# RWKV's decay part of the next head pair is made ahead of this pair's inverse; the next delta head's keys are made under this head's chunk loop

## The chip, the core and the metric

The kernel runs on one NeuronCore of one Trainium2 chip. The metric is the device time of one execution in microseconds (us). The kernel before has a median of 2889.58 us over three runs (2887.1 to 2890.51). The profile that is read here is one execution taken by the hardware profiler; its span, from the first to the last instruction, is 2890.0 us.

## The reference, cut to what matters

One layer of a hybrid encoder works on 512 tokens of width 2048 in float32. One combined input projection feeds two groups of heads; their outputs are concatenated and projected, and cross attention to 256 memory tokens and a squared-ReLU MLP follow.

```python
y = rmsnorm(x) @ W_in                       # one projection for both groups
h = x + concat[GDN(y_gdn), RWKV7(y_rwkv)] @ W_out
h = h + CrossAttn(rmsnorm(h), rmsnorm(mem)) # 4 heads, 256 memory tokens
h = h + relu(rmsnorm(h) @ W_up)**2 @ W_down # hidden 8192
out = rmsnorm(h)

# RWKV-7, 16 heads of 64
w_log = -softplus(-(w0 + tanh(w_lo) @ w2)) - 0.5
decay = exp(-exp(w_log));  a = sigmoid(a0 + a_lo @ a2)
S_t = S_{t-1} (diag(decay_t) + a_t b_t^T) + v_t k_t^T;  o_t = S_t r_t

# gated DeltaNet, 8 heads of 128
q, k, v = silu(conv4(y))                    # q and k are then l2-normed
S_t = exp(g_t) (I - beta_t k_t k_t^T) S_{t-1} + beta_t k_t v_t^T;  o_t = S_t^T q_t
```

Both recurrences are computed in chunks: inside a chunk a unit triangular matrix is inverted, and a short loop over the chunks carries the state.

## The kernel before, in words

**Stages.** The first stage (0 to about 1120 us of the span) makes the input projection, both groups of heads, the key projection of the memory (`kp`) and its product with the query weights (`kq`). Then come the memory's values with the output weights (`vp`, `vo`), the mixer's output projection (`op`), attention (`sc`, `at`) and the MLP (`mxu`, `mgu`, `mmu`, then the tiles that end in `d`). The change lies in the first stage, and one line of it in the MLP.

**Precision.** Each float32 weight tile is split into a rounded part `whi` (ScalarE) and the rest `wlo` (VectorE), and so are the activations (`xhi`, `xlo`). A product then takes three matmuls. An output of the input projection takes 16 x 3 matmuls of 128x128 by 512 columns, tile `py`. There are 59 such outputs: three blocks of low ranks and rates, and then for each of eight rounds j three for a pair of RWKV heads (r, k, v, in this order) and four for one delta head (k, q, v, gate). `evict` (line 541) puts each into one of four buffers `y`, from which the heads take it.

**The order of the work.** It is planned while the program is built. Every piece of work is a Python generator that yields operations; `chain(generator, rank)` adds it to a list. `run` (line 285) repeatedly takes the next operation of each chain, works out by a cost model when it could start on its engine, and issues the one with the smallest start time, to which a rank adds 150 ns a step except on TensorE. `yield after(event)` holds a chain until another has issued the work that adds the event. The result is a fixed order for each engine: on the chip each engine takes its instructions in that order and waits for semaphores. The projections are one chain (`projections`, line 573, rank 4), so their matmuls fill TensorE wherever the heads' chains (rank 3) have nothing ready. `loader` (line 438) fetches weights into three `wraw` buffers over SyncE's DMA queue and splits them. `presums` (line 412, tile `ds`) makes sums of MLP weights ahead of time on VectorE where there is room, until the last `kp` is made.

**A pair of RWKV heads** is `rwkv(j)` (line 858). It begins with the decay part: two matmuls `pW` and `pA` of 64 rows by 512 columns, two Tanh on ScalarE, a scale and a scan (a running sum that restarts every 64 columns) on VectorE, and two Exp that give `E1` and `E2`; `tA` holds the second Tanh. Then k is mixed and normed (`pn`), r and v are mixed, the scaled operands `AR` and `BK` are made once the pair before has issued its output products (`after("po", j - 1)`), the chunk matrices `GA` and `GB` come from `pgA` and `pgB`, and a chain of its own inverts 16x16 blocks on GpSimd (`inverse_blocks`, tiles `sr`, over DRAM buffers `nd` and `bg`). Meanwhile this chain makes transposes and `pak`, `pkv`, and the tile `Qs`; it waits for the inverse (`after("ri", j)`), doubles the blocks twice (tiles `ri`), adds the chain of the next pair (`chain(rwkv(j + 1), 3)`, line 1029) and runs the chunk loop (`rs`) and the output products (`po`, `pp`).

**A delta head** is `gdn(h)` (line 1092). It loads the rates `B` (tile `gqd`), convolves k (three VectorE operations, tile `gk`), makes the decays `EG` and `E` (tiles `gEG`, `gE`) and the normed k (`gkn`, matmuls `gn`), then `pkk` and the matrix for the inverse, which again runs on GpSimd. q, v and the gate follow; after the inverse come the block steps (tiles `gi`), the event `("inverted", h)`, the chunk loop (`gs`), the output products (`gpo`), the output's norm (`gon`) and the store. Only as its last act does it add the chain of the next head (line 1237). `fetch` loads the next head's `E` earlier.

**What hangs on the last head.** The 16 outputs of `kp` come after the last input projection, and the first `kq` waits for the event `("inverted", 7)` (line 616), since `kq` uses PSUM banks that the delta head's block steps use.

Of the kernel before, what the change touches and what calls it, by code (L numbers as in the profile page):

```python
# [12 lines left out]
ALU = mybir.AluOpType  # L13
# [14 lines left out]
for _n, _w in (("ident", 128), ("ones", 128), ("mA", 128),  # L28
               ("lv64", 2 * 64), ("cen", 64), ("sneg", 128), ("mbias", 128),
               ("rst64", 512)):  # L30
    CST[_n] = (_off, _w)
    _off += _w
# [13 lines left out]
def constants():  # L46
    c = np.zeros((P, NCST), np.float32)

    def put(name, a):
        o, w = CST[name]  # L50
        c[:, o:o + w] = a

    i = np.arange(P)
    put("ident", np.eye(P))
    put("ones", 1.0)
    j = np.arange(64)
    st = (j[:, None] < j[None, :]).astype(np.float32)
# [12 lines left out]
    put("rst64", np.tile((np.arange(512) % 64 != 0).astype(np.float32), (P, 1)))  # L70
    return c


def build(tc, I, out):
# [43 lines left out]
    def psb(nm, tag="mx", bufs=2):  # L118
        return tile_of(ps, [P, 512], F32, tag, nm, bufs)
# [162 lines left out]
    def after(*ev):  # L282
        return lambda: ev in events
# [573 lines left out]

    def rwkv(j):
        base = 3 + 7 * j
        js = slice(j * P, (j + 1) * P)  # L860
# [66 lines left out]
        def store(full):  # L927
# [3 lines left out]
        inv = []  # L931
        chain(inverse_blocks(f"ri{j}", store, 16, ("k", "r", "E2"), lambda: (short(), short(240)), lambda: True, inv,
                             True), 1, ("ri", j))
# [36 lines left out]
        for f in (0, 1):  # L970
# [4 lines left out]
                         [prod(1 - h, h, pkv[:, CS[c]], Kt[:, CS[c]], VV[:, CS[c]]) for h, c in (L4 + H4)[:14]])  # L975
        AkV = tl("tA")
# [114 lines left out]

    def gdn(h):
        base = 3 + 7 * h + 3
        gsh = lambda w=512: short(w, "sg")
        c3 = lambda a: a.rearrange("p (c t) -> p c t", t=P)

        def conv(i, s, tag):

            yield after("py", base + i)
            y = ybuf[ys[base + i]]  # L1100
            a = tl(tag)
            cv = lambda i: hconv[:, (s * 8 + h) * 4 + i:(s * 8 + h) * 4 + i + 1]
            yield AC.activation(a, y[:, 0:512], AF.Copy, scale=cv(0))
            for n in range(1, 4):
                yield DV.scalar_tensor_tensor(out=a, in0=y[:, n:n + 512], scalar=cv(n), in1=a,
                                              op0=ALU.mult, op1=ALU.add)
            yfree.append(ys.pop(base + i))
            t = gsh()
            yield AC.activation(t, a, AF.Tanh)
            yield DV.scalar_tensor_tensor(out=a, in0=t, scalar=1.0, in1=a, op0=ALU.add, op1=ALU.mult)  # L1110
            return a

        def normed(x, bias, tag, nm):
            sq = gsh()
            yield AC.activation(sq, x, AF.Square)
            pn = psb(f"gn{h}_{nm}", "mg")
            yield from sums_(pn, onesr, sq)
            yield from rsq_(sq, pn, 1.0, b_eps6, bias)
            xn = tl(tag)
            yield DV.tensor_tensor(out=xn, in0=x, in1=sq, op=ALU.mult)  # L1120
            return xn
# [12 lines left out]
        eg = tl("eg", 4, 2)  # L1134
        yield DV.tensor_copy(eg.unsqueeze(2), c3(EG)[:, :, P - 1:P])
        for c in range(4):
# [15 lines left out]
        def store(full):  # L1152
# [5 lines left out]
                             after("gq", h), inv, moved=True), 1, ("gi", h))  # L1158
        q_ = yield from conv(1, 0, "gq")
        qn = yield from normed(q_, b_lq, "gqn", 1)  # L1160
        wd, qd = tl("gq"), B
# [17 lines left out]
        v_ = yield from conv(2, 2, "gv")  # L1179
        pvt = psb(f"pvt{h}", "mg")  # L1180
# [16 lines left out]
        events.add(("inverted", h))  # L1197
        vns, Ss = tl("gEs"), tl("gEG")
        for c in range(4):
# [35 lines left out]
        yield SL.dma_start(mixd[h], o)  # L1235
        if h < 7:
            chain(gdn(h + 1), 3)

# [694 lines left out]
    def splits():  # L1933
        for u in units:
            if u[0] == "d" and u[1:3] in INSITU and u[1:] not in PRE:
                for i, w in order_of(u):
                    for x in xs(u):
                        yield (after("sum", u, w, x) if isinstance(w, str) else after("raw", u, w, x))
                        r = raws[u, {"s2": A11, "s3": A21, "s4": A11 if u == units[-1] else A12}.get(w, w), x]
                        halves[u, i, x] = hl = yield from take(hfree)  # L1940
                        yield from cut(r, *hl)
                        events.add(("half", u, i, x))
                        if w not in (A11, "s2") and (w != A12 or u == units[-1]):
                            wfree.append(r)
                continue
# [520 lines left out]
```

## Time and profile before

| what | us |
|---|---|
| median of three runs | 2889.58 |
| lowest and highest run | 2887.1, 2890.51 |
| the profiled execution, span | 2890.0 |
| TensorE matmul busy in it | 2862.2 |
| VectorE busy | 2333.9 |
| ScalarE busy | 1571.7 |
| GpSimd busy | 214.7 |
| from first to last `kp` matmul | 907.2 to 1019.9 |
| from first to last `kq` matmul | 1022.3 to 1117.5 |

A matmul's record has a modelled end and overlaps the next one's, so the pitch from start to start says more than the duration. Idle time is counted from the modelled end of the matmul before. Each planner-issued instruction has the line of the helper that issues it (L257), so tiles, not lines, tell what an instruction is.

### The profile page before, as it was taken

The numbers are of one execution on the slowest core, as the hardware profiler recorded it, in microseconds if no ns is written. First come the engines' busy times: TensorE is split into PE (matmuls) and PEld (weight loads), VectorE is DVE, ScalarE is ACT, GpSimd is POOL, SyncE is SP. The second block draws the span as 40 slices with busy tenths as digits, with TensorE's granted clock in tenths as the row PEclk, the third lists the DMA queues.
The fourth block names the chain that finished last, engine by engine and source line by source line (L and its number), as shares of the span: only waits on it lengthen the run. The fifth ranks groups of instructions, "written<-read, shape, count | busy, mean of one in ns | idle before, by whom it ended". The sixth has DMA issues, their size and how long they took to land.

```text
span 2890.0 us, 49168 instructions
## 1 busy us (share of the span) xinstructions
PE 2862.2 (99%) x18794; PEld 2419.1 (84%) x18794; DVE 2333.9 (81%) x3559; ACT 1571.7 (54%) x2233; POOL 214.7 (7%) x539
## 2 busy tenths in 40 slices
PE   9999999999999999999999999999999999999998
PEld 7877887877877888889988888888888888888887
DVE  7787787787877877769956898899998878786888
ACT  6555555645656655664445556555555644454544
POOL 0213213213212100000000000000000000000000
PEclk9999999999999999999999999999999999999999
DMA  5656656657656788784422354666565878887733
GB/s 191 166 147 176 176 149 187 165 154 189 180 161 200 214 257 274 232 292 151 124 95 88 110 164 153 199 195 207 189 200 178 292 249 277 295 257 247 265 101 110
DMA packets 321212, 553.01 MB, mean 191 GB/s; under 512 B 101128, under 2 KB 188428, under 8 KB 320976
## 3 DMA queue, kind: packets, MB, share of 16 engines
q1 hardware_dynamic: 293584, 518.41, 58.7%
q10 hardware_dynamic: 27392, 31.46, 3.1%
q8 instruction: 147, 2.41, 0.3%
q14 instruction: 89, 0.73, 0.1%
HBM read 443.45 MB, written 106.31 MB: 190 GB/s over the span
## 4 chain that ended last, share of the span: by engine, by line
PE 94%; DMA 3%; DVE 1%; ACT 1%; issue 1%; ACTq 0%; SPq 0%; DVEq 0%
PE py L257 22%; PE mxu L257 12%; PE mgd L257 6%; PE mgu L257 6%; PE mxd L257 6%; PE op L122 6%; PE vp L122 3%; PE mmu L257 3%; PE sc L122 3%; PE at L122 3%; PE scrd L257 3%; PE scgd L257 3%; PE mmd L257 3%; PE kq L257 3%; PE kp L257 2%; DMA wraw<-in_wo 1%
## 5 line engine op out<-in xcount | busy, mean ns | idle before, releaser
L257 ACT CAST whi<-wraw 128x1024 fp32r<-128x1024 f32 (+1 forms) x365 | 382.8, 1049 | 370.1 <-PE py L257 138.7
L257 DVE TENSOR_TENSOR wlo<-wraw,whi 128x1024 fp32r<-128x1024 f32 (+1 forms) x365 | 446.8, 1224 | 90.0 <-ACT whi L257 82.5
L257 PE MATMUL py<-xhi,whi 128*128 128x512 f32 x928 | 373.9, 403 | 6.8 <-ACT xhi L257 6.8
L257 PE MATMUL py<-xhi,wlo 128*128 128x512 f32 x928 | 373.1, 402 | 0.0
L257 PE MATMUL py<-xlo,whi 128*128 128x512 f32 x928 | 372.4, 401 | 0.0
L257 ACT CAST whi<-w 128x1024 fp32r<-128x1024 f32 x178 | 187.6, 1054 | 174.0 <-PE scgd L257 42.3
L257 DVE TENSOR_TENSOR wlo<-w,whi 128x1024 fp32r<-128x1024 f32 x178 | 217.3, 1221 | 43.4 <-ACT whi L257 40.9
L257 PE MATMUL mxu<-cb,whi 128*128 128x512 f32 x1016 | 249.3, 392 | 0.0
L257 PEld LDWEIGHTS mxu<-cb,whi 128*128 128x128 f32 x1016 | 184.7, 189 | 34.3
L257 PEld LDWEIGHTS py<-xhi,whi 128*128 128x128 f32 x928 | 175.3, 189 | 42.0 <-ACT xhi L257 6.8
L257 PEld LDWEIGHTS py<-xhi,wlo 128*128 128x128 f32 x928 | 175.3, 189 | 34.7 <-issue 1.0
L257 PEld LDWEIGHTS py<-xlo,whi 128*128 128x128 f32 x928 | 175.3, 189 | 33.8 <-DVE xlo L257 0.5
L131 DVE TENSOR_TENSOR wlo<-wraw,whi 128x1024 fp32r<-128x1024 f32 x112 | 136.7, 1222 | 44.8 <-ACT whi L130 44.3
L130 ACT CAST whi<-wraw 128x1024 fp32r<-128x1024 f32 x112 | 117.6, 1051 | 86.8 <-PE op L122 26.2
L257 PE MATMUL mxu<-cb,wlo 128*128 128x256 f32 x1016 | 142.7, 283 | 0.7 <-DVE wlo L257 0.7
L257 PEld LDWEIGHTS mxu<-cb,wlo 128*128 128x128 f32 x1016 | 135.1, 191 | 6.0 <-DVE wlo L257 0.9
L257 PE MATMUL mgu<-cb,whi 128*128 128x512 f32 x512 | 129.3, 394 | 0.1
L257 PE MATMUL mxd<-whi,cb 128*128 128x512 f32 x512 | 126.8, 389 | 0.0
L257 PE MATMUL mgd<-whi,cb 128*128 128x512 f32 x512 | 126.4, 389 | 0.0
L257 ACT ACT_TABLE_LOAD x87 | 111.6, 1283 | 16.5 <-DVE suml_gon L257 8.6
L122 PE MATMUL op<-ob,whi 128*128 128x256 f32 (+1 forms) x752 | 115.2, 304 | 0.0
L257 ACT CAST whi<-ws 128x1024 fp32r<-128x1024 f32 x75 | 79.0, 1053 | 64.0 <-PE mgu L257 48.1
(943 smaller groups left out, 6429.3 us busy)
## 6 DMA issues: line engine op xcount, KB each, us to landing
wraw<-in_w_in SPq DMA_DIRECT2D x116, 512.0 KB, 4.7
wraw<-in_w_up SPq DMA_DIRECT2D x65, 512.0 KB, 3.6
w<-in_w_up SPq DMA_DIRECT2D x63, 512.0 KB, 4.2
ds<-in_w_dm SPq DMA_DIRECT2D x128, 205.0 KB, 4.4
sd_s<-ds SPq DMA_DIRECT2D x128, 205.0 KB, 4.9
wraw<-sd_s SPq DMA_DIRECT2D x51, 512.0 KB, 4.9
w<-sd_s SPq DMA_DIRECT2D x50, 512.0 KB, 5.5
w<-in_w_dm SPq DMA_DIRECT2D x48, 512.0 KB, 4.9
```

The costliest lines, as they stand in the source:

```text
L122: PE.matmul(o, l, r, start=start, stop=stop, skip_group_check=again)
L130: S.copy(hi, src)
L131: V.tensor_tensor(out=lo, in0=src, in1=hi.bitcast(F32), op=ALU.subtract)
L257: f(*a, **k)
```

## The change

**RWKV.** The decay part becomes a chain of its own, `decay(j)`. `rwkv(j)` takes its results from `heads`, and adds `decay(j + 1)` as soon as it starts. That chain loads its weights `lw` at once and then waits for the event `("room", j + 1)`, which `rwkv(j)` adds after it made `Qs`, ahead of the wait for its inverse. `rwkv(j)` doesn't go on to the block steps before the next pair's two Tanh are issued (`("drawn", j + 1)`). The scan now runs in place, in two halves of 256 columns, with a table `rst64` half as wide; the two short buffers `tw` and `Lg` are gone. So that two pairs can hold these tiles at once, `E2` and `v` swap their places from pair to pair, and `tA` alternates with a new tile `tB`.

**Delta.** The first part of `gdn` becomes `keys(h)`: the convolution of k, the decays and the normed k. `keys(h + 1)` is added after head h's block steps, ahead of its chunk loop. `gdn(h + 1)` is added after the output products, ahead of the output's norm; it loads `B` and waits for `("keys", h + 1)`. The state `Ss` moves from the tile `gEG`, which `keys` now writes, to `gqn`. The tile `kt` waits for the store of the head before (`("gout", h - 1)`).

**MLP.** In `splits`, for the weights whose sums are made in place, the chain goes on after cutting `s1` only once `s2` is issued, which reads `s1`.

The diff, cut to its core:

```diff
-               ("rst64", 512)):
+               ("rst64", 256)):
...
-    def rwkv(j):
-        base = 3 + 7 * j
+    heads = {}
+    tE, tV, tT = (lambda j, a=a: a[j % 2] for a in (("E2", "v"), ("v", "E2"), ("tA", "tB")))
+
+    def decay(j):
         js = slice(j * P, (j + 1) * P)
         lw = tl("lw", P)
         yield SM.dma_start(lw, I["w2a2"][:, js])
         c3 = lambda a: a.rearrange("p (c t) -> p c t", t=64)
         yield after("lowrank")
         yield after("zeros")
+        if j:
+            yield after("room", j)
         pW, pA = psb(f"pW{j}"), psb(f"pA{j}")
         yield [TE.matmul(pW, lw[0:64, :], wa[0:64, :], start=True, stop=True),
                TE.matmul(pA, lw[64:128, :], wa[64:128, :], start=True, stop=True)]
-        tw = short()
-        yield AC.activation(tw, pW, AF.Tanh, scale=0.5, bias=hw0[:, j:j + 1])
-        tA = tl("tA")
+        E2 = tl(tE(j))
+        yield AC.activation(E2, pW, AF.Tanh, scale=0.5, bias=hw0[:, j:j + 1])
+        tA = tl(tT(j))
         yield AC.activation(tA, pA, AF.Tanh, scale=0.5, bias=ha0[:, j:j + 1])
-        yield DV.tensor_scalar(out=tw, in0=tw, scalar1=-0.5 * C, scalar2=-0.5 * C, op0=ALU.mult, op1=ALU.add)
-        Lg = short()
-        yield DV.tensor_tensor_scan(out=Lg, data0=K("rst64"), data1=tw, initial=0.0, op0=ALU.mult, op1=ALU.add)
+        events.add(("drawn", j))
+        yield DV.tensor_scalar(out=E2, in0=E2, scalar1=-0.5 * C, scalar2=-0.5 * C, op0=ALU.mult, op1=ALU.add)
+        for s in (slice(0, 256), slice(256, 512)):
+            yield DV.tensor_tensor_scan(out=E2[:, s], data0=K("rst64"), data1=E2[:, s], initial=0.0,
+                                        op0=ALU.mult, op1=ALU.add)
         E1 = tl("E1", shape=[P, 8, 65])
         yield DV.memset(E1[:, :, 0:1], 1.0)
-        yield AC.activation(E1[:, :, 1:65], c3(Lg), AF.Exp)
-        E2 = tl("E2")
-        yield AC.activation(E2, Lg, AF.Exp, scale=-1.0)
+        yield AC.activation(E1[:, :, 1:65], c3(E2), AF.Exp)
+        yield AC.activation(E2, E2, AF.Exp, scale=-1.0)
+        heads[j] = tA, E1, E2
+        events.add(("head", j))
+
+    def rwkv(j):
...
+        yield after("head", j)
+        tA, E1, E2 = heads.pop(j)
+        if j < 7:
+            chain(decay(j + 1), 3)
         k_ = tl("k")
...
-        v_ = tl("v")
+        v_ = tl(tV(j))
...
         yield DV.tensor_tensor(out=c3(Qs)[:, 1:8], in0=c3(pkv)[:, 0:7],
                                in1=lam[:, 0:7].unsqueeze(2).broadcast_to([P, 7, 64]), op=ALU.mult)
+        events.add(("room", j + 1))
...
         yield after("ri", j)
+        if j < 7:
+            yield after("drawn", j + 1)
...
+    fronts = {}
+
+    def keys(h):
         yield after("rows")
         yield after("zeros")
         if h:
             yield lambda: h in pre
-        E, B = pre.pop(h) if h else tl("gE"), tl("gqd")
+        E = pre.pop(h) if h else tl("gE")
...
-        yield SL.dma_start(B, Rd[32 + h:33 + h, :].broadcast_to([P, T]))
-        k_ = yield from conv(0, 1, "gk")
+        k_ = yield from conv(h, 0, 1, "gk")
         EG = tl("gEG")
         yield AC.activation(EG, E, AF.Exp)
...
         yield AC.activation(E, E, AF.Exp)
-        kn = yield from normed(k_, None, "gkn", 0)
+        kn = yield from normed(h, k_, None, "gkn", 0)
+        fronts[h] = E, EG, eg, kn
+        events.add(("keys", h))
+
+    def gdn(h):
...
+        B = tl("gqd")
+        yield SL.dma_start(B, Rd[32 + h:33 + h, :].broadcast_to([P, T]))
+        yield after("keys", h)
+        E, EG, eg, kn = fronts.pop(h)
         kb = tl("gk")
...
+        if h:
+            yield after("gout", h - 1)
         kt = tl("gkt")
...
         events.add(("inverted", h))
-        vns, Ss = tl("gEs"), tl("gEG")
+        vns, Ss = tl("gEs"), tl("gqn")
+        if h < 7:
+            chain(keys(h + 1), 3)
         for c in range(4):
...
+        if h < 7:
+            chain(gdn(h + 1), 3)
         o = tl("gkt")
...
         yield SL.dma_start(mixd[h], o)
-        if h < 7:
-            chain(gdn(h + 1), 3)
+        events.add(("gout", h))
...
     chain(projections(), 4)
+    chain(decay(0), 3)
     chain(rwkv(0), 3)
+    chain(keys(0), 3)
     chain(gdn(0), 3)
...
                         events.add(("half", u, i, x))
+                        if w == "s1":
+                            yield after("sum", u, "s2", x)
                         if w not in (A11, "s2") and (w != A12 or u == units[-1]):
                             wfree.append(r)
```

More of the change, by code (lines that the diff above doesn't have):

```diff
@@ L69, in constants @@
     put("mbias", np.where(i[:, None] <= i[None, :], 1e30, -1e30))
-    put("rst64", np.tile((np.arange(512) % 64 != 0).astype(np.float32), (P, 1)))
+    put("rst64", np.tile((np.arange(256) % 64 != 0).astype(np.float32), (P, 1)))
     return c
@@ L931, in rwkv @@
         inv = []
-        chain(inverse_blocks(f"ri{j}", store, 16, ("k", "r", "E2"), lambda: (short(), short(240)), lambda: True, inv,
+        chain(inverse_blocks(f"ri{j}", store, 16, ("k", "r", tE(j)), lambda: (short(), short(240)), lambda: True, inv,
                              True), 1, ("ri", j))
@@ L975, in rwkv @@
                          [prod(1 - h, h, pkv[:, CS[c]], Kt[:, CS[c]], VV[:, CS[c]]) for h, c in (L4 + H4)[:14]])
-        AkV = tl("tA")
+        AkV = tl(tT(j))
         for f in (0, 1):
@@ L1090, in fetch @@
         pre[h] = e
[L1092 to L1121, printed above, removed]
@@ new lines, in build, with conv @@
+    gsh = lambda w=512: short(w, "sg")
+    g3 = lambda a: a.rearrange("p (c t) -> p c t", t=P)
+    def conv(h, i, s, tag):
+        yield after("py", 3 + 7 * h + 3 + i)
+        y = ybuf[ys[3 + 7 * h + 3 + i]]
+        a = tl(tag)
+        cv = lambda i: hconv[:, (s * 8 + h) * 4 + i:(s * 8 + h) * 4 + i + 1]
+        yield AC.activation(a, y[:, 0:512], AF.Copy, scale=cv(0))
+        for n in range(1, 4):
+            yield DV.scalar_tensor_tensor(out=a, in0=y[:, n:n + 512], scalar=cv(n), in1=a,
+                                          op0=ALU.mult, op1=ALU.add)
+        yfree.append(ys.pop(3 + 7 * h + 3 + i))
+        t = gsh()
+        yield AC.activation(t, a, AF.Tanh)
+        yield DV.scalar_tensor_tensor(out=a, in0=t, scalar=1.0, in1=a, op0=ALU.add, op1=ALU.mult)
+        return a
@@ L1123, in gdn, with normed @@
+    def normed(h, x, bias, tag, nm):
+        sq = gsh()
+        yield AC.activation(sq, x, AF.Square)
+        pn = psb(f"gn{h}_{nm}", "mg")
+        yield from sums_(pn, onesr, sq)
+        yield from rsq_(sq, pn, 1.0, b_eps6, bias)
+        xn = tl(tag)
+        yield DV.tensor_tensor(out=xn, in0=x, in1=sq, op=ALU.mult)
+        return xn
+    fronts = {}
+    def keys(h):
         yield after("rows")
@@ L1134, in gdn @@
         eg = tl("eg", 4, 2)
-        yield DV.tensor_copy(eg.unsqueeze(2), c3(EG)[:, :, P - 1:P])
+        yield DV.tensor_copy(eg.unsqueeze(2), g3(EG)[:, :, P - 1:P])
         for c in range(4):
@@ L1140, in gdn @@
         yield AC.activation(E, E, AF.Exp)
-        kn = yield from normed(k_, None, "gkn", 0)
+        kn = yield from normed(h, k_, None, "gkn", 0)
+        fronts[h] = E, EG, eg, kn
+        events.add(("keys", h))
+    def gdn(h):
+        c3 = g3
+        base = 3 + 7 * h + 3
+        yield after("rows")
+        yield after("zeros")
+        B = tl("gqd")
+        yield SL.dma_start(B, Rd[32 + h:33 + h, :].broadcast_to([P, T]))
+        yield after("keys", h)
+        E, EG, eg, kn = fronts.pop(h)
         kb = tl("gk")
@@ L1158, in gdn @@
                              after("gq", h), inv, moved=True), 1, ("gi", h))
-        q_ = yield from conv(1, 0, "gq")
-        qn = yield from normed(q_, b_lq, "gqn", 1)
+        q_ = yield from conv(h, 1, 0, "gq")
+        qn = yield from normed(h, q_, b_lq, "gqn", 1)
         wd, qd = tl("gq"), B
@@ L1178, in gdn @@
         events.add(("gq", h))
-        v_ = yield from conv(2, 2, "gv")
+        v_ = yield from conv(h, 2, 2, "gv")
         pvt = psb(f"pvt{h}", "mg")
```

3 lines of the change are left out of this document (added).

## The prediction

> **What bounds the kernel now.** I read the page's totals first, then the busy time of each engine by stage, then who made TensorE wait, then single instructions. The totals:
>
> ```profile
> span 2890.0 us, 49168 instructions
> PE 2862.2 (99%) x18794; PEld 2419.1 (84%) x18794; DVE 2333.9 (81%) x3559; ACT 1571.7 (54%) x2233; POOL 214.7 (7%) x539
> ```
>
> TensorE is busy for 99%, and it matters whether that is work or a modelled end that covers a wait. The busy time by stage (after the window its length, then busy us and instruction count of PE, weight loads, VectorE, ScalarE, GpSimd):
>
> ```profile
> 0.00:50.00 50.00, 43.21 (x174) 34.56 (x175) 36.26 (x67) 33.18 (x50) 2.43 (x11) 1.00 0.70 244
> 50.00:800.00 750.00, 750.00 (x6741) 602.10 (x6740) 587.85 (x1077) 407.85 (x569) 172.00 (x431) 1.00 0.61 166
> 800.00:1120.00 320.00, 310.89 (x2515) 261.42 (x2514) 248.16 (x449) 184.26 (x297) 40.29 (x97) 1.00 0.72 215
> 1120.00:1300.00 180.00, 179.29 (x928) 153.73 (x927) 125.98 (x201) 110.70 (x183) 0.00 (x0) 1.00 0.80 265
> 1300.00:2850.00 1550.00, 1548.97 (x8315) 1342.96 (x8314) 1305.50 (x1724) 815.41 (x1101) 0.00 (x0) 1.00 0.59 191
> 2850.00:2890.00 40.00, 29.83 (x132) 24.38 (x130) 30.17 (x45) 20.32 (x37) 0.00 (x0) 0.92 0.30 105
> ```
>
> The reader is to see where TensorE idles at all: 6.79 us at the start, 0.00 in the 750 us that hold nearly seven of the eight rounds of heads, 9.11 where the heads end, 0.71 and 1.03 later, 10.17 in the output's tail. The change touches neither start nor tail, so all that it can recover is 9.11 + 0.71 + 1.03 = 10.85 us. Who is waited for between 800 and 1120 us (total, times, longest):
>
> ```profile
> PE kp L257 <- DVE wlo L257: 2.7, 1, 2.7
> PE rs L257 <- DVE Qs L257: 2.2, 2, 1.2
> PE gs L257 <- DVE TtG L257: 1.2, 1, 1.2
> PE kq L257 <- DVE y L257: 1.1, 1, 1.1
> PE rs L257 <- DVE BK L257: 0.7, 1, 0.7
> PE ri6s L257 <- DVE k L257: 0.6, 1, 0.6
> PE vp L122 <- DVE y L257: 0.5, 1, 0.5
> ```
>
> These are eight waits with 9.0 us in sum, none of them long, and four of the seven rows are matmuls of the heads. That the busy time is work shows in TensorE's own instructions (start, duration), at the beginning and once it runs:
>
> ```profile
> 9.88 0.63 PE L257 MATMUL py<-xhi,whi 128*128 128x512 f32 x1
> 10.30 0.63 PE L257 MATMUL py<-xlo,whi 128*128 128x512 f32 x1
> ...
> 13.40 0.40 PE L257 MATMUL py<-xhi,whi 128*128 128x512 f32 x1
> 13.63 0.40 PE L257 MATMUL py<-xlo,whi 128*128 128x512 f32 x1
> ```
>
> From 13.40 on the pitch is 0.23 us for 512 columns although each record is 0.40 long; a wait shorter than the difference hides in a record, so the 10.85 may be a little low. The kernel is a stream of TensorE work, and the change removes no matmul. Only waits, and what a switch between kinds of matmul costs, can move the time.
>
> **The decay part.** Per pair it is two matmul instructions (each two records), two Tanh, a scale, a scan and two Exp. All of them stay; the scan becomes two, and their place changes.
>
> ```profile
> L257 PE MATMUL pW<-wa,lw x16: 589/641/693, 58.7 to 828.9; 64*128 64x512 f32 x16
> L257 ACT ACTIVATE sr<-pW,prm x8: 687/688/690, 59.9 to 829.6; 128x512 f32<-128x512 f32 x8
> L257 DVE TENSOR_TENSOR_SCAN sr<-cst,sr x8: 1217/1224/1225, 66.4 to 833.5; 128x512 f32<-128x512 f32 x8
> ```
>
> The new place is between `Qs` and the block steps of the pair before. For pair 6 these rows bound it:
>
> ```profile
> L257 DVE TENSOR_TENSOR Qs<-pkv,lam x2: 620/623/626, 776.5 to 889.3; 128x448 f32<-128x448 f32 x2
> L257 PE MATMUL ri6x<-r,GA x16: 218/218/267, 797.8 to 806.1; 64*64 64x64 f32 x16
> ```
>
> From 777.1 to 797.8 there are 20.7 us in which the pair waits for GpSimd. The moved chain takes, from its last matmul record at 828.9 to the end of the scan at 834.7 and two Exp as long as a Tanh, until 836.1, so 7.2 us today; it fits. Were that cover gone, `drawn` would hold the block steps for two records and two Tanh, 2 x 0.64 + 2 x 0.69 = 2.7 us a pair, on this pair's chain and not on TensorE, which has projections. For the split of the scan, these rows of one round say what a quarter of the columns costs (count, then busy us and mean ns):
>
> ```profile
> L257 DVE SCALAR_TENSOR_TENSOR gk<-y,prm,gk 128x512 f32<-128x512 f32 x3 | 2.2, 748 | 0.1
> L257 DVE SCALAR_TENSOR_TENSOR gE<-gE,RT,cst 128x128 f32<-128x128 f32 x4 | 1.4, 402 | 0.0
> ```
>
> 128 columns take 402 ns where 512 take 748, so a fixed part of (4 x 402 - 748) / 3 = 287 ns. Two half scans cost between 1.22 us (no fixed part) and 2.45 (each as long as the whole); I take 1.5. That is +0.3 us a pair on VectorE, which has 162 free of the 750. The load of `lw` stays one a pair and is issued nearly a round ahead of its use, so no matmul waits for its landing; what stands behind it in SyncE's queue waits for one issue, as it does now.
>
> What does the pair gain? The last of its inputs is v, whose eviction for pair 7 stands here:
>
> ```profile
> 849.22 0.69 DVE L257 TENSOR_TENSOR y<-py,rstd 128x512 f32<-128x512 f32 x1 [0.30 <-PE py L257]
> ```
>
> The decay of pair 7 was done at 836.1, 13.1 us ahead of v. So the chain of pair 7 gains nothing: 0, and if `drawn` holds it, 2.7 us later, beside a TensorE that has work. On TensorE the two matmuls leave the chunk loop, where they had small neighbours, and stand among projections. A visit of small matmuls to the projections costs what these rows show:
>
> ```profile
> 491.21 0.39 PE L257 MATMUL py<-xhi,wlo 128*128 128x512 f32 x1
> 491.53 0.27 PE L257 MATMUL gi3x<-gk,gEs 64*64 64x64 f32 x2
> ...
> 491.77 0.22 PE L257 MATMUL gi3w<-gk,gEs 64*64 64x64 f32 x2
> 491.92 0.50 PE L257 MATMUL py<-xhi,whi 128*128 128x512 f32 x1
> ```
>
> 0.32 instead of 0.23 going in and about 0.1 coming out, 0.2 us a visit. One visit more or fewer in each of eight rounds is +1.6 or -1.6 us; with no reason for either, 0.
>
> **The delta head's keys.** Head 7 ends the stage, so I follow it. Its k convolution may now start after head 6's block steps, but needs k:
>
> ```profile
> L257 PE MATMUL gi6u<-TtG,gkn x8: 218/218/267, 845.0 to 845.4; 64*64 64x64 f32 x8
> L257 PE MATMUL gs<-sg,TtG x6: 271/274/275, 853.4 to 862.3; 128*128 128x128 f32 x6
> 863.53 0.69 DVE L257 TENSOR_TENSOR y<-py,rstd 128x512 f32<-128x512 f32 x1 [0.25 <-PE py L257]
> 884.03 0.72 ACT L257 ACTIVATE gk<-y,prm 128x512 f32<-128x512 f32 x1
> ```
>
> Block steps end at 845.6, the chunk loop at 862.6, k is evicted at 864.2, and the convolution starts at 884.0. So the keys can't come under head 6's chunk loop at all; they come under its output products and norm, at most 884.0 - 864.2 = 19.8 us earlier, at least 0. I take 15, since VectorE is busy there and a part will queue. The load of `B` is issued after `gpo` instead of after the store; it is the same load and runs beside the convolution. The wait for `gout` is met long before `kt`. The three taps and four masked rows of the keys, 2.2 + 1.4 us of VectorE by the rows above, are moved and not added. What 15 us are worth is read where head 7's inverse meets `kq`:
>
> ```profile
> 1018.33 2.00 PE L257 MATMUL kp<-mhl,whi 128*128 128x512 f32 x8
> 1020.26 0.68 PE L257 MATMUL gi7u<-TtG,gkn 64*64 64x64 f32 x8
> 1022.09 0.49 PE L257 MATMUL gs<-gv,TtG 128*128 128x128 f32 x2 [1.16 <-DVE TtG L257]
> ```
>
> The last `kp` and the last block step end together, and the 1.2 us after them have no cover because `kq` may not start. With the inverse 15 us earlier, `kp` covers it: -1.2. Nothing more is to be had there, since TensorE had work until then; a delay, though, would cost one us per us.
>
> **The other waits.** The longest, 2.7 on `kp`'s weights, has its cause in SyncE's queue:
>
> ```profile
> 903.76 3.84 SPq L257 DMA_DIRECT2D E<-bg16U  x4
> 907.70 0.55 SPq L257 DMA_DIRECT2D wraw<-in_wk  x1
> ```
>
> The weights stand behind four reloads of pair 7's inverse. Pair 7 keeps its time (v sets it), so the wait may well stay: between 0 and -2.7, I take -0.7. The waits of `rs` and `ri6s`, 2.2 + 0.7 + 0.6, hang on what VectorE has in front at that moment, and that is dealt anew: 0 to -3.5, I take -1.5. The 1.1 + 0.5 on `y` are `kq`'s own evictions: 0. New waits: at least 0, at most as much as all eight now, 9.0; I take +0.5, since the same planner left none in 50 to 800 us. The line in `splits` delays a cut by at most one sum of 1024 columns, in a stage that idles 1.03 of 1550 us: 0.
>
> The sum: -1.2 - 0.7 - 1.5 + 0.5 = -2.9. From the profiled 2890.0 this is 2887.1; that execution lies 0.4 over the median of 2889.6, so I predict 2886.7 us.
>
> **The rivals.** *The late waits go altogether.* With head 7 off the end of the stage, all heads' and `kp` waits vanish (9.0 - 1.6 = 7.4), and one visit a round is saved (1.6): 2889.6 - 9.0 = 2880.6. For it: each wait is on an engine that the changed chains use. Against: the cause of the 2.7 isn't touched.
>
> *Slower: delta work stands in front of `kp`'s splits.* Up to 907 us projections fill TensorE; after that only `kp` does. Head 7's convolutions move from behind 884 to where VectorE also makes pair 7's operands and `kp`'s `wlo`. If keys and the taps of q and v (2.2 + 1.4 + 2 x 2.2 = 8.0 us of VectorE) come in front of splits that TensorE needs, it waits for them: 2889.6 + 8.0 = 2897.6. It decides from the last projection on: work that is done by then costs nothing. For it: the 2.7 us wait is of this kind. Against: delta work comes earlier, so less of it should be left after 907.
>
> The Trainium skill (TensorE: Matmul & The Clock Gate, Part 1: The HAM clock gate) says that TensorE's clock falls to half after an idle window of about 3.4 us and needs about as long to recover. By that rule a wait of 8 us would cost about eight matmuls at twice the pitch besides. The first matmuls here agree, with a pitch of 0.43 us before 13 us and 0.23 after; at 0.2 us each that would make the rival about 2899. The longest wait of now, 2.7, stays under it.
>
> *It doesn't do what it says.* v still sets the pair and k the delta head, VectorE's queue eats the lead, and the same waits stand elsewhere: 2889.6.
>
> **How the numbers follow.** A measurement of this kernel can't tell less than 0.2% (5.8 us) from no change, so faster is below 2883.8, slower above 2895.4. Forecast 0.43 (its own spread 2883 to 2891, so 0.03 of it counts as faster), late waits gone 0.30, slower 0.16, nothing 0.11. Faster 0.33, same 0.51, slower 0.16. The lower end is all 10.85 us recovered, 2889.6 - 10.85 = 2878.8, so 2879; the upper end takes in most but not all of the slower case: 2896.
>
> **What would show it.** Right: `kq` starts without the wait for `TtG`; head 7's `gk` convolution starts near 865 to 870 and `gi7u` ends near 1005; `pgA` of pair 7 stays within some 3 us; TensorE stays at 750.00 of 750; the idle of 800 to 1120 us falls to about 6. Wrong: idle inside the rounds, a wait on `wlo` over 3 us after 900, a changed matmul count, or the idle of the MLP above 3 us.

## The result, and the profile after

The changed kernel takes 2912.92 us (median of four runs, 2908.84 to 2914.05); the kernel before, run beside it, 2890.05. The ratio is 1.0074, 95% interval 1.0059 to 1.0089: slower by about 0.7%, outside the predicted range. The profiled execution after has a span of 2912.2 us against 2890.0, so 22.2 us have to be found. A trace shows one execution, and executions of one kernel lie 3 to 11 us apart here, so a difference of a few us between two traces need not come from an edit.

The totals of the page after:

```profile
span 2912.2 us, 49151 instructions
PE 2870.2 (99%) x18794; PEld 2423.0 (83%) x18794; DVE 2330.7 (80%) x3567; ACT 1569.2 (54%) x2233; POOL 198.6 (7%) x539
```

The matmul count is unchanged. The busy time by stage of the kernel after, with the columns of the prediction's table (the column after GpSimd is the granted TensorE clock):

```profile
50.00:800.00 750.00, 750.00 (x6707) 601.72 (x6706) 582.36 (x1082) 406.79 (x571) 162.59 (x431) 1.00 0.55 159
800.00:1120.00 320.00, 305.49 (x2490) 255.36 (x2489) 238.19 (x434) 177.26 (x282) 33.54 (x97) 0.98 0.69 209
...
1300.00:2850.00 1550.00, 1539.42 (x8272) 1334.55 (x8272) 1295.65 (x1718) 811.84 (x1102) 0.00 (x0) 1.00 0.60 195
```

The rounds (50 to 800) still idle 0.00. Two stages got worse: 800 to 1120 us idles 14.51 instead of 9.11, and the MLP 10.58 instead of 1.03. The waits of TensorE over the whole run say at what (the `py` row is the start, as before):

```profile
PE kp L257 <- ACT mhl L257: 9.0, 2, 6.5
PE scrd L257 <- ACT whi L257: 8.3, 1, 8.3
PE py L257 <- ACT xhi L257: 7.4, 1, 7.4
```

In both places the clock falls too. The windows that the granted clock's records of the kernel after mark off:

```profile
905.00:923.20 18.20, 13.33 (x152) 10.91 (x150) 10.74 (x20) 11.15 (x18) 5.51 (x18) 1.00 0.90 227
923.20:933.40 10.20, 5.04 (x30) 3.50 (x34) 6.52 (x11) 3.31 (x5) 4.79 (x14) 0.50 0.64 216
...
2720.00:2752.70 32.70, 28.75 (x127) 23.46 (x125) 25.62 (x38) 13.66 (x17) 0.00 (x0) 1.00 0.57 174
2752.70:2762.90 10.20, 5.87 (x14) 4.61 (x15) 3.68 (x3) 4.18 (x4) 0.00 (x0) 0.50 1.02 383
```

TensorE is busy for 5.04 and 5.87 us at half clock. The same work at full clock would take about half as long (a pitch of 0.43 against 0.23 us, by the first matmuls in the prediction), so I estimate the cost at 2.5 and 2.9 us. So the loss is in two lumps. The opening of `kp` idles 11.1 us of the 55 from 905 to 960 where the kernel before idles 2.8: with the clock, 8.3 + 2.5 = 10.8. The MLP loses 10.58 - 1.03 + 2.9 = 12.5. Together 23.3, and the waits that went (`TtG`, 1.2, and smaller ones) lie against it.

**The first lump** is a supply that comes late. The opening of `kp` needs 16 pieces of the memory, split into tiles `mhl`, eight from `wraw` and eight from `mraw`. ScalarE's part of these splits, the row of the kernel before and then, in the next fence, of the kernel after:

```profile
L257 ACT ACTIVATE mhl<-mraw,prm x8: 493/499/509, 906.9 to 916.4; 128x256 fp32r<-128x256 f32 x8
```

```profile
L257 ACT ACTIVATE mhl<-mraw,prm x8: 492/499/504, 910.8 to 928.8; 128x256 fp32r<-128x256 f32 x8
```

The last one starts 12.4 us later. What stands between them is in ScalarE's order after (start, duration):

```profile
905.29 0.63 ACT L257 ACTIVATE sg<-gq 128x512 f32<-128x512 f32 x1 [0.76 <-DVE gq L257]
906.48 1.31 ACT L257 ACTIVATE mhl<-wraw,prm 128x256 fp32r<-128x256 f32 x3
907.81 1.28 ACT L257 ACT_TABLE_LOAD   x1
909.10 0.69 ACT L257 ACTIVATE sg<-gn,cb_e 128x512 f32<-128x512 f32 x1
...
913.01 1.28 ACT L257 ACT_TABLE_LOAD   x1
914.31 0.73 ACT L257 ACTIVATE sg<-sg,cb_lq 128x512 f32<-128x512 f32 x1
914.94 1.03 ACT L257 CAST whi<-wraw 128x1024 fp32r<-128x1024 f32 x1
915.88 0.90 ACT L257 ACTIVATE mhl<-mraw,prm 128x256 fp32r<-128x256 f32 x2
924.33 1.04 ACT L257 CAST whi<-wraw 128x1024 fp32r<-128x1024 f32 x1 [7.55 <-DMA wraw<-in_wk]
```

The Tanh, the square and the norm of head 7's query, with two table loads, now stand among the memory's splits; in the kernel before that query came after them, at 931. (Two table loads stood among the splits there too, at 897.60 and 901.20, for the norm of head 7's key.) And at 916.8 ScalarE stops for 7.55 us, at a cast whose weights have not landed, with three splits behind it. SyncE's queue after shows why they are late:

```profile
909.75 0.55 SPq L257 DMA_DIRECT2D wraw<-in_wk  x1
910.80 0.81 SPq L257 DMA_DIRECT2D sd_s<-ds  x2
912.07 0.33 SPq L257 DMA_DIRECT2D sgi<-ndgi  x1
912.50 1.22 SPq L257 DMA_DIRECT2D sd_s<-ds  x2
916.07 1.78 SPq L257 DMA_DIRECT2D ds<-in_w_dm  x2
917.95 0.38 SPq L257 DMA_DIRECT2D wraw<-in_wk  x1
```

A piece of the presums (stores of `ds`, then the reload of the same tiles) stands in front of the weights; in the kernel before only one store lies between these two loads:

```profile
908.59 0.33 SPq L257 DMA_DIRECT2D sd_s<-ds  x1
909.44 21.25 SPq L257 DMA_DIRECT2D wraw<-in_wk  x8
```

The first of them is in the prediction's rows, at 907.70.

**The second lump** is a debt. The loads of `ds` in stage 1, four to a piece, of the kernel before and, in the next fence, of the kernel after:

```profile
L257 SPq DMA_DIRECT2D ds<-in_w_dm x160: 327/383/1734, 74.1 to 1024.6; - x160
```

```profile
L257 SPq DMA_DIRECT2D ds<-in_w_dm x148: 327/383/2069, 74.6 to 1018.5; - x148
```

So 37 pieces of sums are made instead of 40, since the presums fill what room the order leaves and end with the last `kp`. The MLP makes up what is missing, and its last stores now stand directly in front of the loads that read them (SyncE after; `sl` is the tile in which the MLP makes sums):

```profile
2742.66 3.19 SPq L257 DMA_DIRECT2D sd_s<-sl  x3
2746.26 0.32 SPq L257 DMA_DIRECT2D sd_s<-acc  x1
...
2749.59 1.52 SPq L257 DMA_DIRECT2D wraw<-sd_s  x3
```

In the kernel before the last such store is at 2623.5 and these loads start at 2718.66. The matmuls of `scrd` wait for them until 2757.03.

### The profile page after: what moved, and what is told of

Read it like the earlier page. It is cut to its first block, busy times and chain, and to the rows that moved or that the text cites. A ratio compares the mean times of both kernels' runs of the same rounds, so it can differ in the third digit from the quotient of the medians.

```text
span 2912.2 us, 49151 instructions
## 1 busy us (share of the span) xinstructions
PE 2870.2 (99%) x18794; PEld 2423.0 (83%) x18794; DVE 2330.7 (80%) x3567; ACT 1569.2 (54%) x2233; POOL 198.6 (7%) x539
## 4 chain that ended last, share of the span: by engine, by line
PE 92%; DMA 3%; DVE 2%; ACT 1%; issue 1%; ACTq 0%; SPq 0%; DVEq 0%
PE py L257 23%; PE mxu L257 12%; PE mgd L257 6%; PE mgu L257 6%; PE mxd L257 6%; PE op L122 5%; PE vp L122 3%; PE scrd L257 3%; PE scgd L257 3%; PE mmu L257 3%; PE sc L122 3%; PE at L122 3%; PE mmd L257 3%; PE kq L257 2%; PE kp L257 2%; PE vo L122 1%
## 5 line engine op out<-in xcount | busy, mean ns | idle before, releaser
L257 PE MATMUL mxd<-whi,cb 128*128 128x512 f32 x488 | 120.8, 389 | 0.9 <-ACT whi L257 0.9
L257 PEld LDWEIGHTS mgd<-whi,cb 128*128 128x128 f32 x512 | 96.1, 188 | 19.9
```

The costliest lines, as they stand in the source:

```text
L257: f(*a, **k)
```

## The experiments

My first theory had these two lumps as separate, the first from the piece of presums in the queue, the second from the three missing pieces. All kernels below were timed beside the kernel before.

**1. The missing sums, put back and taken away.** The first kernel lets the presums of the changed kernel go on until 40 pieces are made:

```diff
-  chain(presums([...], PIECE, after("kp", 15)), ...)
+  chain(presums([...], PIECE, lambda: npiece[0] >= 40), ...)
```

> Changed kernel, but the presums go on until 40 pieces of sums are made, as many as the kernel before makes, where the changed kernel ends them with the last kp column after 37; nothing is left out. Theory (the MLP's late stall comes from the pieces of sums that stage 1 no longer makes): the wait of scrd for whi, 8.28 us in the changed kernel, is gone (longest wait of that stage under 3 us), the last sl store of sums lies near 2625 us instead of 2746, and the time falls by about 12 us to 2901 (2897 to 2904); the 6.50 us wait in kp stays. Rival (the MLP's stall comes from the new guard in splits or from something else in the MLP's order): the wait stays near 8 us and the time near 2913.

The second does the opposite to the kernel before: `npiece[0] >= 37`.

> Kernel before with the presums ended after 37 pieces instead of 40, and with the guard in splits (which leaves the order of the kernel before as it is); RWKV and the delta heads are as before, and the missing sums are made in the MLP. Theory (missing sums alone make the late stall): a wait of 6 to 9 us appears in the MLP's last units near 2740, the clock is granted at half behind it, and the time rises by 8 to 14 us to about 2902. Rival (the stall needs the moved decay and keys): no wait over 3 us after 1300, time 2890 within 3 us.

Measured: 2904.84 us with 40 pieces (1.0046, 1.0033 to 1.0059), and 2902.49 for the kernel before with 37 (1.0039, 1.0026 to 1.0051). In the first the waits of the MLP are gone and 1300 to 2850 us idles 1.04; the gain in the medians is 8 us instead of 12. In the traces the last `kq` starts 1.7 us later (1130.3 instead of 1128.6) and the last `scrd` 9.9 us earlier (2854.0 instead of 2863.9), so from there on 11.6 us are won. The 1.7 us are there before the added pieces come, since the first `kp` already starts at 910.8 instead of 909.1. In the second this wait is there, in a kernel that is otherwise the one before:

```profile
PE scrd L257 <- ACT whi L257: 10.2, 1, 10.2
```

Its MLP costs 14.2 us more (the last `scrd` starts 11.3 us late where the stage before it was 2.9 early). So the missing sums make the second lump without any help from the moved work; 5 shows in what way. The line in `splits`, added by itself to the kernel before, leaves every engine's instructions in the same order.

**2. The piece in the queue.** The changed kernel, with the 34th piece held until `kp` column 3 is done; then the same with 40 pieces.

```diff
+  if npiece[0] == 33:
+      yield after("kp", 3)
   yield from presum(...)
```

> Changed kernel, but the presums' 34th piece, whose four loads stand in SyncE's queue between the second and the fourth load of wk, waits until kp column 3 is done; 37 pieces as before, nothing is left out. Theory (the kp stall is the wk load held up on SyncE's queue by the reload of ds, which waits for its own store): the waits of kp for mhl fall from 10.0 us to under 3, kp ends 8 to 11 us earlier, no granted clock of 0.5 near 925, and the time falls to about 2902 (2899 to 2906), the MLP's wait of 8.28 us staying. Rival (the delta keys' and inverse's own work on VectorE and ScalarE, or the earlier inverse's reloads in the queue, hold up the memory tokens): kp's wait stays above 5 us and the time near 2913.

> Both edits on the changed kernel: the 34th piece waits for kp column 3, and the presums go on until 40 pieces; nothing is left out. Theory (two separate stalls, one from the queue in kp and one from the missing sums, make up the whole loss): both long waits are gone, no clock at 0.5, and the time is 2887 to 2892, that of the kernel before or some 3 us under it. Rival (the loss is in the moved work itself): 2900 or above.

Measured: 2910.01 us (1.0062, 1.0049 to 1.0076) and 2907.11 (1.0053, 1.0041 to 1.0066). The theory held for a part only. The waits of `kp` for the memory's pieces shrink from 10.0 to 5.5 us in the first kernel. Its splits end at the same time:

```profile
L257 ACT ACTIVATE mhl<-mraw,prm x8: 491/499/504, 915.4 to 928.9; 128x256 fp32r<-128x256 f32 x8
```

But this execution took 2914.07 us, 4 more than the median, and comes to `kp` 4.6 us later (913.7 instead of 909.1), and up to there TensorE's order is that of the changed kernel. Counted from the first `kp`, the last split starts after 15.2 us instead of 19.7. In the second kernel the reload is gone from in front of the weights and the four stores stay; ScalarE's cast waits half as long:

```profile
919.82 1.04 ACT L257 CAST whi<-wraw 128x1024 fp32r<-128x1024 f32 x1 [3.79 <-DMA wraw<-in_wk]
```

The waits of `kp` for pieces are 4.6 us there, and the last split starts at 922.7. The two edits together are still no better than the sums alone: `kq` and `vp` now wait 4.0 and 2.6 us for `whi`, where they waited 0.2 and nothing with the sums alone. That this comes from the pieces that were put off is likely, and not shown.

**3. Each half of the change alone.** The decay half is `decay` with what hangs on it, and the delta heads as before; the delta half is `keys` with what hangs on it, and `rwkv` as before. What each adds to the list of chains:

```diff
+            chain(decay(j + 1), 3)
...
+    chain(decay(0), 3)
```

```diff
+            chain(keys(h + 1), 3)
...
+    chain(keys(0), 3)
```

> The decay half of the change alone (decay made ahead, rst64 of 256, the tiles swapped, the room and drawn waits) with the delta heads as in the kernel before; it makes 40 pieces of sums, as the kernel before. Theory (the loss is in the delta half: its keys ahead put head 7's work into the opening of kp and leave fewer pieces of sums): no wait over 4 us in kp or in the MLP, time 2890 within 4 us. Rival (the decay half costs, by its drawn wait or the E2 it holds longer): 2896 or above.

> The delta half of the change alone (keys ahead under the chunk loop, with the guard in splits) with RWKV as in the kernel before; it makes 35 pieces of sums in stage 1, and no ds reload stands among the first six loads of wk in SyncE's queue. Theory (missing sums make the late stall): scrd's wait in the last part of the MLP is 8 us or more with the clock at half behind it, so 2900 or above by that alone. On the kp stall the theories part: if the ds reload in the queue makes it, kp's waits for mhl stay under 4 us and kp ends within 3 us of the kernel before; if head 7's earlier key work on ScalarE and VectorE makes it, the splits of the memory end near 928 again and kp ends 8 to 16 us later than before.

Measured: the decay half 2920.38 us (1.0098, 1.0084 to 1.0112), the slowest of all, against my theory; the delta half 2911.86 (1.007, 1.0057 to 1.0082). The delta half, with 35 pieces, waits 13.2 us in `scrd`, as the debt says, but has no stall in the opening of `kp` at all:

```profile
905.00:960.00 55.00, 54.69 (x532) 46.81 (x530) 44.00 (x74) 34.30 (x56) 15.33 (x31) 1.00 0.71 212
```

In this order head 7's query is convolved from 918.1 on, behind the memory's splits (904.3 to 909.3); in the changed kernel from 901.6, in front of them. The keys ahead are thus not enough for the stall. Two things differ: where the query falls, and SyncE's queue, where from 909.67 on four loads of weights leave with no piece of the presums between them. The first gave the theory tested in 5; the second is tested in 4.

The decay half loses its time in another place, in front of `kp`. VectorE's order there, and TensorE's wait:

```profile
815.13 1.64 DVE L257 TENSOR_TENSOR_SCAN v<-cst,v 128x256 f32<-128x256 f32 x2
...
818.74 2.33 DVE L257 SCALAR_TENSOR_TENSOR gk<-y,prm,gk 128x512 f32<-128x512 f32 x3 [1.95 <-ACT gk L257]
821.10 0.69 DVE L257 TENSOR_TENSOR y<-py,rstd 128x512 f32<-128x512 f32 x1
```

```profile
821.84 0.79 PE L257 MATMUL py<-xhi,whi 128*128 128x512 f32 x1 [7.17 <-DVE y L257]
```

The eviction of a projection stands on VectorE behind the moved decay of pair 7 and the taps of a delta head, and TensorE's next projection waits for it. That is the longest wait; `kp` begins 27 us late (934.5 instead of 907.2), TensorE idles 16.1 us from 800 to 935 where the kernel before idles 2.4 up to 908, and the rest of the delay was not taken apart. Head 7's own k convolution comes at 929.8, 45 us after that of the kernel before. Why the delta heads fall so far behind when the decay is made ahead and their own keys are not was not tested; it stays open.

**4. Head 7 late, and no sums at all.** The first kernel starts head 7 (keys and rest) where the kernel before does, heads 1 to 6 ahead; the second holds the 32nd piece and all that follow until `kp` column 3. Both make 40 pieces.

```diff
-  if h < 7:
+  if h < 6:
       chain(keys(h + 1), 3)
...
-  if h < 7:
+  if h < 6:
       chain(gdn(h + 1), 3)
...
   events.add(("gout", h))
+  if h == 6:
+      chain(keys(7), 3)
+      chain(gdn(7), 3)
```

> Changed kernel with 40 pieces of sums, in which the keys of head 7 alone, and head 7 itself, start where they start in the kernel before, behind head 6's mixd store; heads 1 to 6 are made ahead as in the change. Theory (head 7's moved work, with what it places in the queues, keeps ScalarE, VectorE and SyncE from the memory's splits at the opening of kp): the eight splits from mraw end near 918 as before instead of 928.8, kp ends within 3 us of the kernel before, and the time is 2887 to 2893. Rival (the opening is late for another reason, the decay or the sums): kp's stall stays and the time is 2901 or above.

> Changed kernel with 40 pieces of sums, where the 32nd piece and all behind it wait until kp column 3 is done: from about 885 us to kp 3 no operation, store or load of the sums is in any queue, while head 7's work stays as early as in the change. If the sums' traffic is the whole cause of the kp stall, kp ends within 3 us of the kernel before, and the time is 2888 to 2893; if head 7's key work takes the rest, the splits of the memory still end 4 us or more late, kp ends 5 us or more late, and the time is 2896 to 2904.

Measured: 2901.08 us (1.0031, 1.0019 to 1.0042) and 2909.64 (1.0065, 1.0052 to 1.0079). Neither is back at 2890. With head 7 late the splits end at 921.8 and the wait is 3.1 us, for `wlo`; the first lump shrinks and does not vanish. With no sums in the queues the waits for `mhl` do vanish (1.1 us in all), although head 7's query stays as early as in the changed kernel: its convolution starts on ScalarE at 899.4, its two table loads at 907.29 and 912.49. The weights now leave SyncE's queue without stores or a reload in front, no cast waits for them, and the splits end 10 us earlier:

```profile
907.52 0.77 SPq L257 DMA_DIRECT2D wraw<-in_wk  x1
909.86 0.34 SPq L257 DMA_DIRECT2D sgi<-ndgi  x1
910.88 18.21 SPq L257 DMA_DIRECT2D wraw<-in_wk  x6
```

```profile
L257 ACT ACTIVATE mhl<-mraw,prm x8: 493/498/506, 910.2 to 918.9; 128x256 fp32r<-128x256 f32 x8
```

So the query's work on ScalarE is not what stalls `kp`; the sums are. Their additions on VectorE are held here too, but the cast's wait for the load (7.55 us with the whole piece in front, 3.79 with its stores alone, none here; the kernel before has one of 3.41 at 913.29, with no wait of `kp` for pieces behind it) says that it is the queue. The opening, 905 to 960, idles 4.0 us instead of 11.1. But the sums that were put off come back one stage later:

```profile
PE vp L122 <- DVE wlo L131: 8.3, 2, 4.3
```

**5. The query behind the splits.** The changed kernel, where head 7 alone waits before its query convolution until the memory is split:

```diff
+  if h == 7:
+      yield lambda: len(mhl) == 16
   q_ = yield from conv(h, 1, 0, "gq")
```

> Changed kernel in which head 7 alone waits with its query convolution, and what follows it, until all 16 pieces of the memory are split; 35 pieces of sums are then made in stage 1, and up to the second load of wk the queues stand as in the changed kernel. Theory (in the changed kernel head 7's query convolution and norm, at 901 to 907 us and with their two table loads, stand on ScalarE among the memory's splits, and the ds reload then falls into the gap on SyncE): the eight splits from mraw end near 918 instead of 929, kp's waits for mhl sum to 4 us or less, no half clock near 925, and kq ends 6 to 12 us earlier than in the changed kernel; the MLP's wait stays or grows (35 pieces), to about 13 us, so the time is 2904 to 2912. Rival (the opening is late for the queues' other work): the splits still end after 925 and kq ends within 3 us of the changed kernel.

Then the same, with the MLP's left sums made earlier: their gate opens with the first down unit and their rank is 1 instead of 4.

```diff
-  chain(leftover(left, ..., lambda d: phase() in (1, 2, 3, 5) or phase() >= d), lambda eng: 4)
+  chain(leftover(left, ..., lambda d: phase() >= 1), lambda eng: 1)
```

> The same with head 7's query held back, and with the sums that stage 1 leaves made earlier in the MLP: their gate opens with the first down unit and the planner ranks them in front (1 instead of 4), so that their last store stands some 40 entries ahead of the last unit's loads in SyncE's queue instead of just in front of it. Theory (not the number of missing sums but the lateness of the last of them makes the MLP's stall): scrd's wait falls below 3 us, and with the kp stall gone too the time is 2884 to 2894. Rival (the missing sums cost their VectorE and DMA time wherever they are made): the MLP loses 8 us or more all the same, 2897 or above.

Measured: 2908.39 us (1.0053, 1.004 to 1.0066) and 2891.39 (0.9996, 0.9988 to 1.0005). With the query held, the splits end 2 us after those of the kernel before, no matmul of `kp` waits for them, and the last `kq` starts at 1115.7 (before 1117.5, after 1128.6):

```profile
L257 ACT ACTIVATE mhl<-mraw,prm x8: 493/506/510, 907.4 to 918.4; 128x256 fp32r<-128x256 f32 x8
```

The order of SyncE's queue changed with it: the presums' reload now comes after the weights, and only two stores stand between them. So this run moves the query and clears the queue at once, and 4 has shown that clearing the queue is enough with the query left early. What the query does is thus indirect: with it early, the planner puts the piece of sums in front of the weights. That it comes about in this way is argued from the change of order, and no run has the query late with the whole piece still in front. The MLP, which now lacks five pieces, waits 14.0 us. In the second kernel the same five pieces are made, only earlier, and this wait is gone:

```profile
800.00:1120.00 320.00, 314.54 (x2554) 265.28 (x2554) 241.56 (x439) 183.84 (x295) 37.94 (x97) 0.99 0.69 207
1300.00:2850.00 1550.00, 1548.97 (x8315) 1342.92 (x8314) 1315.41 (x1740) 814.75 (x1101) 0.00 (x0) 1.00 0.60 196
```

It was thus not the number of sums left, but that the last of them came late. The whole loss is recovered, and with it undone the change is worth nothing that can be measured. The kernel before gains nothing measurable from the same order of the MLP with 37 or 35 pieces, as 6 shows.

**6. Is there something to gain without the change?** In 1, stage 1 with 37 pieces ended 2.9 us earlier than with 40. The kernel before with 37 and with 35 pieces and the left ones early in the MLP:

> Kernel before with the presums ended after 37 pieces (as in the run that showed a 14 us loss in the MLP), and with the left sums made earlier in the MLP in the same way. Theory: the MLP's stall is gone, and what the shorter stage 1 gained (kq ended 2.9 us earlier with 37 pieces than with 40) stays, so 2885 to 2890. Rival (the sums cost in the MLP wherever they stand): 2897 or above.

> Kernel before with the presums ended after 35 pieces instead of 37, and the left sums early in the MLP as in the run before it. It asks whether a shorter list of sums in stage 1 is itself worth time. If stage 1 gains by each piece that leaves it (37 pieces ended kq 2.9 and 5.5 us earlier than 40 in two runs), kq ends 5 to 9 us before that of the kernel before and the time is 2882 to 2887; if what 37 pieces gained was the order that the planner happened on, the time is 2887 to 2893. In neither case a wait of scrd over 3 us.

Measured: 2890.20 us (0.9995, 0.9986 to 1.0003) and 2889.34 (0.9987, 0.9978 to 0.9996). The last `kq` starts at 1112.0 and 1118.1, but the first is from an execution of 2886.91 us and the second from one of 2894.56, so these two traces can't tell whether fewer pieces shorten stage 1; the medians show no gain from it. The second may be about 0.1% under the kernel before, which is less than what I counted as a difference. No version beats the kernel before by more than that.

## Why the prediction was wrong, point by point

- **What bounds the kernel** was right: 18794 matmuls before and after, and the loss that was found is all waits of TensorE and its clock.
- **The decay part at 0** was right for this change: the rounds idle 0.00, `pgA` of pair 7 starts at 869.6 instead of 868.1. The split scan takes 2 x 0.68 = 1.36 us; I took 1.5. But the price named for a lost cover, 2.7 us "and not on TensorE, which has projections", has the wrong bearer: in the run with this half alone TensorE waited 7.17 us, because evictions of those same projections stand on VectorE behind the moved operations. I had not named what is queued there.
- **The keys' lead** was right in kind: head 7's k convolution is at 867.5 on VectorE, as "865 to 870" said, and the wait for `TtG` is gone. `gi7u` moved further than forecast, to 985.4 rather than to about 1005. The gain of 1.2 us came as worked out.
- **"Against: delta work comes earlier, so less of it should be left after 907"** is, with the next point, the step that failed for the first lump. Earlier work isn't work that is over: the lead carried head 7's query from 931 to 901, in front of the memory's splits, and with it the order of SyncE's queue changed, which I had not followed. There a piece of the presums came in front of a load of weights; the cast waits 7.55 us for it, and the splits behind the cast keep TensorE. The slower rival was nearest to the truth: its place, `kp`'s opening, was right. Its size (8.0 us forecast, 8.3 of added idle measured) agrees by chance, since its mechanism was another: not delta work on VectorE in front of `wlo`, but sums in SyncE's queue in front of weights. With the query left early and the sums taken out, the waits for the memory's pieces fell from 10.0 to 1.1 us.
- **"New waits: ... at most as much as all eight now, 9.0; I take +0.5"** failed as a term and as a bound: +0.5 stood for what became 10.8 us in the opening of `kp`. The sum of the waits of a tuned order says nothing about those of another order; the single waits of 6.5 and 8.3 us are each larger than any of those eight.
- **"The line in `splits` ... 0"** was right for the line and wrong as the only term of the MLP. No step counted the presums, although they fill exactly the room that a changed order leaves and end with the last `kp`. Three pieces fewer cost 12.5 us more than a thousand us later: the largest single term, and absent from the sum. The cost is not the work itself but that it comes just in front of the loads that read it; made earlier in the MLP, it costs nothing that shows. Of the prediction's own signs of being wrong this one came: the MLP's idle above 3 us, at 10.58.
- The Trainium skill (TensorE: Matmul & The Clock Gate, Part 1: The HAM clock gate) gave a penalty on top of a wait of that length. The trace agrees that it falls to half: at 0.50, from 4.0 us after the beginning of the wait of 8.28 us (2748.75 to 2757.03) until 5.9 us after its end. The recovery was thus longer than the about 3.4 us that I took from the Trainium skill, whose row gives one busy window of that length as the least; and the slowed work cost 2.5 and 2.9 us at the two places, by the estimate above, where the prediction allowed 1.6 for one.

## What to carry to other kernels

Where a planner fixes the order at build time, an edit changes the whole order, so cost what fills the gaps (here sums of weights for a later stage) as well as what is moved: count it before and after, and look where the debt is paid. The filler's own transfers stand in the queues too, and can come in front of something urgent. When a chain is moved earlier, follow every part of it to where it lands, and ask on each in-order engine and queue what now stands behind it at the next tight spot. And the sum of all waits of a tuned kernel is no upper bound for the waits of its successor.

## What the runs showed of the hardware

The spells of half clock between 50 us and the output's tail had, over all the traces of this case, lengths of 3.4, 6.8, 10.2, 13.7 and 17.1 us, that is one to five times 3.4. A wait of 14.02 us brought the longest (window of the kernel with the query held back, around the wait of `scrd` that ends at 2748.85):

```profile
2736.90:2754.00 17.10, 5.15 (x12) 4.08 (x13) 5.24 (x10) 2.37 (x3) 0.00 (x0) 0.50 0.92 313
```

The spell covers most of the wait and 5.15 us of work. A spell also came with shorter idling: in the kernel before with 37 pieces TensorE was busy for 1.46 of 3.40 us, and the next 3.4 us ran at half clock:

```profile
911.20:914.60 3.40, 1.46 (x12) 1.22 (x11) 1.54 (x2) 1.85 (x3) 0.00 (x0) 1.00 0.85 294
914.60:918.00 3.40, 3.40 (x42) 2.96 (x42) 2.40 (x5) 2.80 (x4) 0.00 (x0) 0.50 0.52 171
```

So 1.94 us of idling cost, by the same estimate, another 1.7, half of 3.4. It need not: the kernel before has a wait of 2.71 us (in the prediction's rows) and no such spell in that stage.
